# Weight sums moved into the attention on GpSimd, and the up projection's products tied in their emitted order

## The chip, the cores and the metric

The kernel runs on one core of a Trainium2 chip. The metric is the device time of one execution in microseconds (us), the median of several runs. An engine is named as in the profile: PE is TensorE, DVE is VectorE, ACT is ScalarE, POOL is GpSimd, SP issues the transfers. A name such as L191 is a line of the kernel before; the rows of the changed kernel's order carry that kernel's own lines, and the text says which line of before they answer to.

## The reference

One layer of a decoder trunk over 1040 tokens (16 learned ones and 1024 given ones) of 1024 features:

```python
h = layer_norm(concat([meta, x]))
proj = h @ w_in
q_lat, kv_lat, k_pe, z, xbc, dt_raw, g_attn, g_ssd = split(proj)
y_attn = mla_branch(q_lat, kv_lat, k_pe, ...)     # 8 heads, softmax(q k) v, then @ w_o
y_ssd  = ssd_branch(z, xbc, dt_raw, ...)          # chunked state-space scan, then @ w_o_ssd
mixed  = sigmoid(g_attn) * y_attn + sigmoid(g_ssd) * y_ssd
h = layer_norm(ALPHA * h + mixed @ w_out)
u = causal_dwconv(h @ w_up)                        # D_FF = 2816: 22 gate and 22 value tiles of 128
gate, val = split(u)
h = layer_norm(ALPHA * h + (silu(gate) * val) @ w_down)
return h[:, 16:]
```

All inputs are float32. Every large product is made of three products of rounded parts (a high and a low part of each operand: high by high, low by high, high by low).

## The kernel before, in words

The kernel runs through stages one after the other: embedding norm and latents (0 to 155 us of the span), the attention (to 541), the gate stage (to 752), the state-space stage (to 1420), its output products and the merged output product (to 1751), the up projection (to 2232) and the down projection. Activations lie with features on the 128 partitions and tokens along the free axis. Instructions are written per stage in Python; a scheduler then sets each engine's order from their emitted order, their priorities and the tiles that are free. An engine runs its own list strictly in that order, and SP issues nearly all transfers in one list.

**Attention.** Eight heads (`hd`), three column chunks of 348 tokens (`c`). For each of these 24 units `scores` makes the score tiles in PSUM, the maximum (L571), the exponential on ACT, and scales the tile `p` on DVE (L589); the last block of a tile is filled with zeros on GpSimd (L593, a memset). `weighted` of the unit before transposes the `p` tiles on PE (L611) and multiplies them with the values (L617). The head's weights are loaded (`wraw<-wk`, `wraw<-wqb`) and split by ACT and DVE.

**Gate stage.** For each of eight blocks `m`: `o_proj` and `gate` (L698 on DVE) with their products on PE; after block 2 `dt_chain`, which for three chunks runs a chain of some 16 small DVE instructions on a 64-partition tile `q` (L719 to L733, one buffer), and ends in three transposes of `q` on PE (L736); `h_centered`, a column sum of eight tiles on DVE (L760) with one product on PE (L762); and `down_sums`, called two at a time. `down_sums(j)` (L738 to L749), for 11 values of `j`, loads two 512 KB blocks of the down projection's weights (tiles `tw1`, `tw2`, one buffer each), makes four differences of 128x512 on DVE and stores both blocks again (`t13_d[j]`, `t42_d[j]`). Only the down projection reads them.

**Up projection.** It is a blocked product with seven products (q = 1 to 7) of half size in place of eight. `prod(ps, q, w)` is one of them: 24 matmuls of 128x258 or 128x256 (L191) into a PSUM pair `d`. The right operands are forms of the normalized activations, four tiles each: `T1`, `T2`, `T3`, `T4`, `B2` for q = 5, 6, 7, 4, 3; each form is a cast on ACT (L199) and a difference on DVE (L200). The left operands are made per tile pair `f` (22 of them) by `wrest(f)`: two weight loads of 512 KB, four sums `s1` to `s4` of 128x512 on GpSimd (L1108 to L1111), and splits by ACT and DVE. `first(f)` calls `wrest` and issues product 6 of the first four `f` (products 1 and 2 of these stand earlier, beside the norm), with `u2 = p1 + d` on DVE (L1148); the loop over `f` then emits products 7, 5, 3, 4. In between stand the convolution steps on DVE and ACT (`conv_up`, L1131 and L1133).

**The norm before it.** `rs` is a list of eight tiles of the residual (`r` in the rows). The lines from L1191 on make `T2` (with the temporary tile `t2`), then `rs[j] = rs[j+4] - rs[j]` (L1196) and the forms `T3`, `T1`, `B2`; then four blocks `b21` are loaded back from DRAM (`b<-h_d`), reduced by `t2` on GpSimd (L1205), and formed into `T4`. Then `first(0)` and the loop.

## Time and profile before

| | |
|---|---|
| time, median of 3 runs | 2474.98 us (2471.23 to 2476.71) |
| the profiled execution's own time | 2476.96 us |
| its span, first to last instruction | 2474.9 us |
| mean granted TensorE clock | 0.986 of full speed |
| PE busy | 2379.6 us (96%), 16319 matmuls |
| DVE busy | 1746.3 us (71%), 3945 instructions |
| ACT busy | 1137.5 us (46%) |
| POOL busy | 202.2 us (8%), 190 instructions |
| chain that ended last | PE 80%, DVE 8%, DMA 6%, issue 2%, ACT 2%, POOL 1% |

The span is 2.06 us shorter than the execution's time; that rest lies before the first and after the last instruction. Shares are means over the whole span, so they say little of one stage. A PE window of 62 us in the up projection that holds no idle time has 516 matmuls.

### The profile page before, as it was taken

How to read it: one execution, taken by the hardware profiler on the slowest of the kernel's cores; microseconds unless marked ns; L12 is line 12 of the kernel's file. 1: busy time of each engine (PE TensorE's matmuls, PEld its weight loads, DVE VectorE, ACT ScalarE, POOL GpSimd, SP SyncE). 2: the span in 40 equal slices, each digit the busy share in tenths (PEclk: the TensorE clock that was granted, in tenths of full speed). 3: DMA queues.
4: the chain of work that ended last, by engine and by line, in shares of the span. 5: the costliest groups of instructions: out<-in, count | busy, mean ns of one | idle time of the engine just before them, and what ended most of it. 6: DMA issues, size and time to landing. Idle time of an engine off the chain costs nothing.

```text
span 2474.9 us, 42581 instructions
## 1 busy us (share of the span) xinstructions
PE 2379.6 (96%) x16319; PEld 2252.3 (91%) x16319; DVE 1746.3 (71%) x3945; ACT 1137.5 (46%) x2481; POOL 202.2 (8%) x190
## 2 busy tenths in 40 slices
PE   6999999999999999999999999999789999999996
PEld 5998988989999999999999999999789999998885
DVE  6467667676767678776877744855778777766858
ACT  5335545562226555445554432432544444445443
POOL 0000000000000000000000000202332222210004
PEclk9999999999999999999999999999899999999998
DMA  6120110147792312222212254644322222229332
GB/s 205 47 66 29 42 38 26 46 137 254 246 308 85 101 64 87 82 79 89 84 64 82 66 176 139 212 154 148 116 86 81 83 83 81 78 85 304 123 111 98
DMA packets 124620, 277.29 MB, mean 112 GB/s; under 512 B 14720, under 2 KB 49792, under 8 KB 122368
## 3 DMA queue, kind: packets, MB, share of 16 engines
q1 hardware_dynamic: 124416, 274.57, 33.8%
q8 instruction: 128, 2.10, 0.3%
q14 instruction: 76, 0.62, 0.1%
HBM read 209.62 MB, written 62.80 MB: 110 GB/s over the span
## 4 chain that ended last, share of the span: by engine, by line
PE 80%; DVE 8%; DMA 6%; issue 2%; ACT 2%; POOL 1%; SPq 0%; DVEq 0%; ACTq 0%; POOLq 0%
PE d L191 25%; PE g L171 11%; PE g L173 11%; PE g L172 11%; PE g L1339 5%; PE c L617 3%; PE c L1339 2%; PE c L908 2%; PE c L611 1%; PE c L932 1%; PE c L912 1%; DMA yl<-y_d 1%; DMA tw<-wdl 1%; DMA wraw<-wup 1%; DVE wl L161 1%
## 5 line engine op out<-in xcount | busy, mean ns | idle before, releaser
L191 PE MATMUL d<-f,wh 128*128 128x258 f32 (+1 forms) x4000 | 655.5, 286 | 28.2 <-DVE u L1148 15.7
L191 PEld LDWEIGHTS d<-f,wh 128*128 128x128 f32 x4000 | 558.7, 192 | 31.0 <-ACT wh L199 20.0
L171 PE MATMUL g<-h,wh 128*128 128x348 f32 (+3 forms) x1560 | 508.0, 326 | 4.7 <-ACT lat L399 4.7
L172 PE MATMUL g<-h,wl 128*128 128x348 f32 (+3 forms) x1560 | 507.4, 325 | 0.0
L173 PE MATMUL g<-h,wh 128*128 128x348 f32 (+3 forms) x1560 | 507.0, 325 | 0.0
L191 PE MATMUL d<-f,wl 128*128 128x258 f32 (+1 forms) x2000 | 407.6, 285 | 6.1 <-DVE wl L200 4.3
L191 PEld LDWEIGHTS d<-f,wl 128*128 128x128 f32 x2000 | 314.4, 192 | 7.9 <-DVE wl L200 5.5
L171 PEld LDWEIGHTS g<-h,wh 128*128 128x128 f32 x1560 | 295.4, 189 | 7.4 <-ACT lat L399 5.0
L172 PEld LDWEIGHTS g<-h,wl 128*128 128x128 f32 x1560 | 295.8, 190 | 2.7 <-issue 2.7
L173 PEld LDWEIGHTS g<-h,wh 128*128 128x128 f32 x1560 | 295.1, 189 | 2.7 <-issue 2.7
L161 DVE TENSOR_TENSOR wl<-wraw,wh 128x512 fp32r<-128x512 f32 (+2 forms) x278 | 193.6, 698 | 142.1 <-ACT wh L160 138.9
L160 ACT CAST wh<-wraw 128x512 fp32r<-128x512 f32 (+2 forms) x278 | 167.1, 604 | 254.8 <-PE d L191 122.6
L171 PE MATMUL g<-a,wh 128*128 128x348 f32 (+2 forms) x456 | 149.2, 328 | 1.9 <-DVE kn L200 1.1
L172 PE MATMUL g<-a,wl 128*128 128x348 f32 (+2 forms) x456 | 148.1, 325 | 0.0
L173 PE MATMUL g<-a,wh 128*128 128x348 f32 (+2 forms) x456 | 147.8, 324 | 0.0
L200 DVE TENSOR_TENSOR wl<-wraw,wh 128x512 fp32r<-128x512 f32 x136 | 99.6, 741 | 60.3 <-ACT wh L199 60.2
L199 ACT CAST wh<-wraw 128x512 fp32r<-128x512 f32 x136 | 82.7, 617 | 106.5 <-DMA wraw<-wup 48.9
L813 DVE SCALAR_TENSOR_TENSOR xc<-g,V,xc 128x347 f32<-128x347 f32 (+2 forms) x180 | 103.5, 576 | 33.0 <-ACT xc L809 30.2
L898 ACT ACTIVATE G<-ac,tok 116x116 f32<-116x116 f32 x288 | 91.6, 379 | 42.5 <-PE c L908 42.5
L1339 PE MATMUL g<-wh,dh 128*128 128x512 f32 x352 | 110.7, 396 | 0.0
L1133 DVE SCALAR_TENSOR_TENSOR va<-u,V,va 128x512 f32<-128x512 f32 x88 | 94.8, 1077 | 20.4 <-ACT va L1131 19.1
L199 ACT CAST wh<-s 128x512 fp32r<-128x512 f32 x88 | 53.9, 617 | 88.2 <-PE d L191 45.6
(306 smaller groups left out, 4216.0 us busy)
## 6 DMA issues: line engine op xcount, KB each, us to landing
wraw<-win SPq DMA_DIRECT2D x65, 512.0 KB, 3.4
wraw<-wup SPq DMA_DIRECT2D x48, 512.0 KB, 3.4
ac<-cs_d SPq DMA_DIRECT2D x16, 1044.0 KB, 5.7
wraw<-wos SPq DMA_DIRECT2D x32, 512.0 KB, 3.9
tw<-wdl SPq DMA_DIRECT2D x22, 512.0 KB, 4.6
t_d<-tw SPq DMA_DIRECT2D x22, 512.0 KB, 3.1
gv<-gv_d SPq DMA_DIRECT2D x44, 256.0 KB, 5.9
wraw<-t_d SPq DMA_DIRECT2D x44, 256.0 KB, 3.4
```

The source lines that it names most:

```text
L160: nc.scalar.copy(h[:, :n * ncol], r)
L161: nc.vector.tensor_sub(l[:, :n * ncol], r, f32(h[:, :n * ncol]))
L171: nc.tensor.matmul(ps, ah, bh, start=(k == 0), stop=False)
L172: nc.tensor.matmul(ps, al, bh, start=False, stop=False)
L173: nc.tensor.matmul(ps, ah, bl, start=False, stop=(k == n - 1))
L191: ins = nc.tensor.matmul(ps[:, PO + c0:PO + c1], a, b[:, c0:c1], start=(start and k == 0 and i == 0), stop=(k == n - 1 and i == 2), skip_g ...
L199: nc.scalar.copy(H, src)
L200: nc.vector.tensor_sub(L, src, f32(H))
L813: nc.vector.scalar_tensor_tensor(t[:, l:n], ps[:, hal + l - s:hal + n - s], vec("cw", (3 - s) * 24 + ct), t[:, l:n], ALU.mult, ALU.add)
L898: nc.scalar.activation(G_[:, k * S:(k + 1) * S], ac[:S, hh, C0[b] + k * S:C0[b] + (k + 1) * S], AF.Relu, bias=tok[:, 3 * b + k, 32 + hd:33 ...
L1133: nc.vector.scalar_tensor_tensor(t, src[:, 2 - k:HN - k], vec("fw", (2 - k) * 44 + ti), t, ALU.mult, ALU.add)
L1339: nc.tensor.matmul(pss[t], a[:, o], b, start=(first and j == 0 and i == 0), stop=(j == KH - 1 and i == 2), skip_group_check=not first)
```

## The change

It has three parts.

First, `down_sums` leaves the gate stage and is called in the attention, in each second unit, on GpSimd in place of DVE, with a pool of its own of two buffers per tile. Loads, stores, sums and their number (11 times two loads, four differences, two stores) are the same.

Second, `prod` ties each product behind the one emitted before it (`issue_after`), so that the scheduler can't mix or exchange products; in the loop `first` of a later `f` is emitted just ahead of product 3. The split weights of q = 4 change pool with those of q = 3, and `u2`, `u4` lie in another pool than the rest.

Third, the forms of the second norm are made in their order of use: `T3`, then the loads of `b21` into tiles that the residual leaves free, `T1` with the `b21` differences on DVE in place of GpSimd, then `first(0)`, and only then `B2` and `T4`.

```diff
@@ -642,6 +642,21 @@
                 split(H[:, :n], L[:, :n], of[:, :n])
                 oh[k][c] = (H[:, :n], L[:, :n])
+    pds = eB.enter_context(pool("DS", 2))
+
+    def down_sums(j):
+
+        x, y = (pds.tile([P, D], F32, name=k, tag=k) for k in ("tw1", "tw2"))
+        nc.sync.dma_start(x, wdl[j])
+        nc.sync.dma_start(y, wdl[j + KH])
+        (b11, b12), (b21, b22) = ((t[:, :512], t[:, 512:]) for t in (x, y))
+        nc.gpsimd.tensor_sub(b11, b12, b11)
+        nc.gpsimd.tensor_sub(b12, b22, b12)
+        nc.gpsimd.tensor_sub(b22, b22, b11)
+        nc.gpsimd.tensor_sub(b21, b21, b22)
+        nc.sync.dma_start(t13_d[j], x)
+        nc.sync.dma_start(t42_d[j], y)
+
     last = None
     for hd in range(HEADS):
@@ -657,6 +672,9 @@
                     others()
             if c == 0 and hd % 2 == 0:
                 vt = values(hd // 2)
+            unit = 3 * hd + c
+            if unit % 2 == 0 and unit // 2 < KH:
+                down_sums(unit // 2)
             last = (hd, c, Pt, vt)
     weighted(*last)
@@ -735,19 +753,6 @@
                 for k in range(3):
                     nc.tensor.transpose(tp[:S, k * 64:(k + 1) * 64], q[:, k * S:(k + 1) * S], ident[:64, :64])
                 nc.scalar.copy(tok[:, 3 * c:3 * c + 3, :], tp[:S, :192].rearrange("p (a b) -> p a b", b=64))
-        def down_sums(j):
-
-            x, y = (p3.tile([P, D], F32, name=k, tag=k) for k in ("tw1", "tw2"))
-            nc.sync.dma_start(x, wdl[j])
-            nc.sync.dma_start(y, wdl[j + KH])
-            (b11, b12), (b21, b22) = ((t[:, :512], t[:, 512:]) for t in (x, y))
-            nc.vector.tensor_sub(b11, b12, b11)
-            nc.vector.tensor_sub(b12, b22, b12)
-            nc.vector.tensor_sub(b22, b22, b11)
-            nc.vector.tensor_sub(b21, b21, b22)
-            nc.sync.dma_start(t13_d[j], x)
-            nc.sync.dma_start(t42_d[j], y)
-
         def h_centered(c):
             n = C1[c] - lo(c)
@@ -779,9 +784,6 @@
             gate(B_GA, m, m1_d, yat)
             if m == 2:
                 dt_chain()
-            for j in range(2 * m - 2, 2 * m):
-                if 0 <= j < KH:
-                    down_sums(j)
             if m > 2 and m - 3 < 3:
                 h_centered(m - 3)
             if m + 3 < KT:
@@ -975,7 +977,9 @@
     eF = ctx.enter_context(ExitStack())
     pf1 = eF.enter_context(pool("F1", 16))
     eD = ctx.enter_context(ExitStack())
-    p = eD.enter_context(pool("Dr", 1, "right"))
+    prr = eD.enter_context(pool("Dr", 8, "right"))
+    eT = ctx.enter_context(ExitStack())
+    p = eT.enter_context(pool("Dt", 1, "right"))
     eM = ctx.enter_context(ExitStack())
     pyh = eM.enter_context(pool("Dy", 33, "right"))
     pm = eM.enter_context(pool("Dm", 17, "right"))
@@ -1013,7 +1017,7 @@
     wm = p.tile([P, KT, 1], F32, name="wm", bufs=1)
     for k in range(KT):
         for q in range(2):
-            raw = dtmp("wr", "r", 8)
+            raw = ftile(prr, F32)
             nc.sync.dma_start(raw[:, :512], wor[k][:, 512 * q:512 * q + 512])
             nc.vector.reduce_sum(wm2[:, k, q:q + 1], raw[:, :512], axis=AX.X)
     nc.vector.tensor_add(wm, wm2[:, :, 0:1], wm2[:, :, 1:2])
@@ -1059,7 +1063,7 @@
             W = load_w(wout[m], KT, center=wm)
             ps = dpair()
             mm3h(ps, W, mix)
-            r, hr = dtmp("r", "r", 8), dtmp("hr", "ml", 3)
+            r, hr = ftile(prr, F32), dtmp("hr", "ml", 3)
             nc.sync.dma_start(hr, hc_d[m][:, cols(hi)])
             nc.vector.scalar_tensor_tensor(r, hr, ALPHA, half(ps), ALU.mult, ALU.add)
             if m == 0:
@@ -1072,7 +1076,7 @@
     eM.close()
     pf2 = eF.enter_context(pool("F2", 40))
     p0 = eF.enter_context(pool("E0", 1))
-    pz = eD.enter_context(pool("Dz", hB, "right"))
+    pz = eT.enter_context(pool("Dz", hB, "right"))
@@ -1113,17 +1117,24 @@
             if w is None:
                 r.update({1: wsplit(wp, a11, 4), 2: wsplit(wp, a12, 4)})
             for q, a in ((4, a22), (7, s3), (6, s2), (5, s1), (3, s4)):
-                r[q] = wsplit(p0, a, 4) if q in (7, 6, 3) else wsplit(pe[0], a, 3)
+                r[q] = wsplit(p0, a, 4) if q in (4, 7, 6) else wsplit(pe[0], a, 3)
             return r
+    order = []
+
     def prod(ps, q, w, start=True):
-        return mm3h(ps, w[q], rhs[q], start)
+
+        with tc.issue_after(order[0]) if order else ExitStack():
+            ins = mm3h(ps, w[q], rhs[q], start)
+        order[:] = [ins.ins]
+        return ins
     pe = []
     def etile(name, bufs):
-        return (p0 if name in ("p1", "c11") else pe[0]).tile([P, HN], F32, name=name, tag=name, bufs=bufs)
+        pl = p0 if name in ("p1", "c11") else pe[0] if name in ("u2", "u4") else pe[1]
+        return pl.tile([P, HN], F32, name=name, tag=name, bufs=bufs)
     def conv_up(src, ti, tag, bufs):
@@ -1195,26 +1206,28 @@
     for j in range(hB):
         nc.vector.tensor_sub(rs[j], rs[j + hB], rs[j])
         T3[j] = form(pf2, rs[j])
+    b21 = []
+    for j in range(hB):
+        b21.append(ftile(prr, F32))
+        nc.sync.dma_start(b21[j], h1_d[j + hB][:, cols(0)])
     for j in range(hB):
         T1[j] = form(pf2, b11[j])
     for j in range(hB):
+        nc.vector.tensor_sub(b21[j], b21[j], t2[j])
+    rhs.update({5: T1, 6: T2, 7: T3})
+    eT.close()
+    pe.append(eF.enter_context(pool("E1", 1)))
+    first(0)
+    for j in range(hB):
         B2[j] = form(pf2, rs[j + hB])
     for j in range(hB):
-        b21 = dtmp("b21", "r", 8)
-        nc.sync.dma_start(b21, h1_d[j + hB][:, cols(0)])
-        nc.gpsimd.tensor_sub(b21, b21, t2[j])
-        T4[j] = form(pf2, b21)
-    rhs.update({3: B2, 4: T4, 5: T1, 6: T2, 7: T3})
-
+        T4[j] = form(pf2, b21[j])
+    rhs.update({3: B2, 4: T4})
     eD.close()
-    pe.append(eF.enter_context(pool("E1", 1)))
-    first(0)
+    pe.append(eF.enter_context(pool("E2", 1)))
     begun = 1
     for f in range(NFF):
         q = st[f]
-        while begun < min(NHEAD, f + 2):
-            first(begun)
-            begun += 1
         w, x0, p1 = q["w"], q["x0"], q["p1"]
         x2 = dpair()
         prod(x2, 7, w)
@@ -1237,7 +1250,7 @@
             nc.scalar.copy(u4, half(x0))
         nc.vector.tensor_add(u4, u4, half(x2))
         vb = conv_up(u4, f + NFF, "va", 2)
-        while begun < min(NFF, f + (3 if f + 1 < NHEAD else 2)):
+        if begun < NFF:
             first(begun)
             begun += 1
         prod(x0, 3, w, False)
```

How the orders move, in the attention, the gate stage and the up projection. In these rows the names carry buffer numbers, which differ between the two kernels.

**GpSimd in the attention.** Before, its list holds only the memsets of the `p` tiles:

```order
L593 MEMSET p_2011 111x107
L593 MEMSET p_2030 111x112
L593 MEMSET p_2300 115x1
L593 MEMSET p_2346 115x2
L593 MEMSET p_2584 111x107
L593 MEMSET p_2603 111x112
```

In the changed kernel the differences of `down_sums` (L653 to L656, L744 to L747 of before) stand between them:

```order
L653 TENSOR_TENSOR tw1_2839<-tw1_2839 128x512
L654 TENSOR_TENSOR tw1_2839<-tw2_2840,tw1_2839 128x512
L593 MEMSET p_2313 115x1
L653 TENSOR_TENSOR tw1_3475<-tw1_3475 128x512
L593 MEMSET p_2359 115x2
L654 TENSOR_TENSOR tw1_3475<-tw2_3476,tw1_3475 128x512
L655 TENSOR_TENSOR tw2_3476<-tw2_3476,tw1_3475 128x512
L656 TENSOR_TENSOR tw2_3476<-tw2_3476 128x512
L653 TENSOR_TENSOR tw1_3791<-tw1_3791 128x512
L654 TENSOR_TENSOR tw1_3791<-tw2_3792,tw1_3791 128x512
L593 MEMSET p_2607 111x107
L655 TENSOR_TENSOR tw2_3792<-tw2_3792,tw1_3791 128x512
```

The memset that was the fourth of the list (`p_2346`, now `p_2359`) has 13 differences ahead of it, and all 44 stand ahead of the list's 10th memset (each head has four).

**SP in the attention**, the changed kernel, from the first stores of `down_sums` (L657, L658) on:

```order
L657 DMA t13_d0_122<-tw1_2143 128x1024
L658 DMA t42_d0_133<-tw2_2144 128x1024
L147 DMA wraw_2469<-wk 128x256
L147 DMA wraw_2508<-wqb 128x768
L651 DMA tw2_2460<-wdl 128x1024
L650 DMA tw1_2839<-wdl 128x1024
L651 DMA tw2_2840<-wdl 128x1024
L657 DMA t13_d1_123<-tw1_2459 128x1024
L658 DMA t42_d1_134<-tw2_2460 128x1024
L657 DMA t13_d2_124<-tw1_2839 128x1024
L658 DMA t42_d2_135<-tw2_2840 128x1024
L147 DMA wraw_3029<-wqb 128x768
```

The weights of the next heads (`wraw<-wk`, `wraw<-wqb`, L147) stand behind these stores, which wait for GpSimd. Before, nothing but loads and the stores of head results stood there.

**DVE in the gate stage**, at `dt_chain`'s second chunk (`q` is its tile; `tw1`, `tw2` are those of `down_sums`), before:

```order
L745 TENSOR_TENSOR tw1_8342<-tw2_8343,tw1_8342 128x512
L161 TENSOR_TENSOR wl_8242<-wraw_8235,wh_8241 128x512
L698 SCALAR_TENSOR_TENSOR ga_8011<-ga_8011,ya_7520 128x344
L719 TENSOR_SCALAR q_8057<-w_8056 64x348
L746 TENSOR_TENSOR tw2_8343<-tw2_8343,tw1_8342 128x512
L721 SCALAR_TENSOR_TENSOR q_8057<-q_8057,w_8056 64x348
L747 TENSOR_TENSOR tw2_8343<-tw2_8343 128x512
L721 SCALAR_TENSOR_TENSOR q_8057<-q_8057,w_8056 64x348 x6
L722 SCALAR_TENSOR_TENSOR q_8057<-q_8057,u_8055 64x348
```

and in the changed kernel (L737 to L739 answer to L719 to L721, L716 to L698):

```order
L716 SCALAR_TENSOR_TENSOR ga_8047<-ga_8047,ya_7580 128x334
L716 SCALAR_TENSOR_TENSOR ga_8076<-ga_8076,ya_7607 128x348
L161 TENSOR_TENSOR wl_8312<-wraw_8309,wh_8311 128x512
L737 TENSOR_SCALAR q_8151<-w_8150 64x348
L739 SCALAR_TENSOR_TENSOR q_8151<-q_8151,w_8150 64x348
L161 TENSOR_TENSOR wl_8316<-wraw_8309,wh_8315 128x512
L716 SCALAR_TENSOR_TENSOR ga_8105<-ga_8105,ya_7634 128x344
L739 SCALAR_TENSOR_TENSOR q_8151<-q_8151,w_8150 64x348 x6
L740 SCALAR_TENSOR_TENSOR q_8151<-q_8151,u_8149 64x348
```

The chain no longer has differences with loads ahead of it or in it; on PE its transposes now stand 11 matmuls earlier than before.

**DVE at the start of the up projection**, before, from the last `T1` forms on (then `B2` and `T4`):

```order
L200 TENSOR_TENSOR f_20951<-f_20866,f_20950 128x514
L200 TENSOR_TENSOR f_20955<-f_20868,f_20954 128x514
L200 TENSOR_TENSOR f_20959<-r_20364,f_20958 128x514
L200 TENSOR_TENSOR f_20963<-r_20431,f_20962 128x514
L200 TENSOR_TENSOR f_20967<-r_20498,f_20966 128x514
L200 TENSOR_TENSOR f_20971<-r_20565,f_20970 128x514
L200 TENSOR_TENSOR f_20978<-b21_20974,f_20977 128x514
L200 TENSOR_TENSOR f_20985<-b21_20981,f_20984 128x514
L200 TENSOR_TENSOR f_20992<-b21_20988,f_20991 128x514
L200 TENSOR_TENSOR f_20999<-b21_20995,f_20998 128x514
L1148 TENSOR_TENSOR u2_21064<-p1_20618,d_21039 128x514
L200 TENSOR_TENSOR wl_21020<-wraw_21009,wh_21019 128x512
```

and in the changed kernel (L1216 is the `b21` difference, L1159 answers to L1148):

```order
L200 TENSOR_TENSOR f_20946<-f_20304,f_20945 128x514
L1216 TENSOR_TENSOR f_20949<-f_20949,t2_20884 128x514
L200 TENSOR_TENSOR f_20958<-f_20869,f_20957 128x514
L1216 TENSOR_TENSOR f_20951<-f_20951,t2_20897 128x514
L200 TENSOR_TENSOR f_20962<-f_20871,f_20961 128x514
L1216 TENSOR_TENSOR f_20953<-f_20953,t2_20910 128x514
L200 TENSOR_TENSOR f_20966<-f_20873,f_20965 128x514
L1216 TENSOR_TENSOR f_20955<-f_20955,t2_20923 128x514
L200 TENSOR_TENSOR f_20970<-f_20875,f_20969 128x514
L200 TENSOR_TENSOR f_21042<-f_20371,f_21041 128x514
L1159 TENSOR_TENSOR u2_21039<-p1_20625,d_21014 128x514
L200 TENSOR_TENSOR wl_21007<-s1_20986,wh_21006 128x512
L200 TENSOR_TENSOR wl_21011<-s4_20989,wh_21010 128x512
```

`u2` now stands ahead of the last three `B2` forms and of the `T4` forms. On PE, before, product 6 of f = 0 (into `d_21039`) is followed by its products 5 and 3, and 7 (`d_21125`) comes after these:

```order
L191 MATMUL d_21039<-f_20919,wh_21027 128x258
L191 MATMUL d_21039<-f_20919,wh_21027 128x256
L191 MATMUL d_21039<-f_20942,wh_21031 128x258
...
L191 MATMUL d_21039<-f_20955,wh_21031 128x258
L191 MATMUL d_21039<-f_20955,wh_21031 128x256
L191 MATMUL d_21039<-f_20958,wh_21035 128x258
L191 MATMUL d_21039<-f_20958,wh_21035 128x256
...
L191 MATMUL d_21125<-f_20923,wh_21023 128x258
L191 MATMUL d_21125<-f_20923,wh_21023 128x256
```

In the changed kernel product 6 (`d_21014`) is followed by 7 (`d_21077`), then 5, then product 6 of f = 1 (`d_21170`):

```order
L191 MATMUL d_21014<-f_20926,wh_21002 128x258
L191 MATMUL d_21014<-f_20926,wh_21002 128x256
L191 MATMUL d_21077<-f_20930,wh_20998 128x258
...
L191 MATMUL d_21077<-f_20946,wh_20998 128x258
L191 MATMUL d_21077<-f_20946,wh_20998 128x256
L191 MATMUL d_21014<-f_20957,wh_21006 128x258
L191 MATMUL d_21014<-f_20957,wh_21006 128x256
...
L191 MATMUL d_21170<-f_20886,wh_21158 128x258
L191 MATMUL d_21170<-f_20886,wh_21158 128x256
```

Products 3 and 4 of f = 0 follow behind that.

## Rows read from the trace of the kernel before

**Rows 1.** Windows of 62 us, core 0, from the output product to the up projection.

```profile
core 0: us, PE busy (x) PEld busy (x) DVE busy (x) ACT busy (x) POOL busy (x), PEclk, DMA share, GB/s
1736.00:1798.00 62.00, 45.25 (x355) 44.16 (x354) 48.96 (x77) 34.39 (x58) 16.69 (x8) 0.85 0.33 111
1798.00:1860.00 62.00, 53.03 (x415) 51.18 (x414) 47.50 (x62) 24.88 (x40) 23.49 (x16) 0.99 0.23 77
1860.00:1922.00 62.00, 59.78 (x481) 59.44 (x480) 50.34 (x66) 29.06 (x47) 18.29 (x13) 0.97 0.28 94
1922.00:1984.00 62.00, 62.00 (x516) 62.00 (x515) 48.01 (x63) 29.88 (x49) 16.65 (x12) 1.00 0.25 77
```

**Rows 2.** TensorE's waits by line waited for, whole span: total, times, longest.

```profile
PE d L191 <- DVE u L1148: 15.7, 1, 15.7
...
PE c L736 <- DVE q L733: 3.6, 2, 3.4
...
PE c L762 <- DVE hs L760: 2.1, 1, 2.1
```

**Rows 3.** Windows of 10 us in the gate stage, columns as in Rows 1.

```profile
630.00:640.00 10.00, 6.64 (x35) 6.23 (x34) 8.86 (x21) 2.27 (x5) 0.00 (x0) 0.79 0.74 247
640.00:650.00 10.00, 10.00 (x58) 10.00 (x57) 7.65 (x13) 1.88 (x4) 0.00 (x0) 0.87 0.60 227
660.00:670.00 10.00, 10.00 (x66) 10.00 (x65) 4.44 (x11) 2.48 (x5) 0.00 (x0) 1.00 0.96 309
700.00:710.00 10.00, 7.94 (x42) 7.22 (x41) 5.71 (x12) 1.88 (x4) 0.00 (x0) 0.88 0.85 275
```

**Rows 4.** Timeline of the gate stage, VectorE: start, length, idle before and releaser.

```profile
624.10 0.69 DVE L744 TENSOR_TENSOR tw<-tw 128x512 f32<-128x512 f32 x1 [3.37 <-DMA tw<-wdl]
...
628.70 0.33 DVE L719 TENSOR_SCALAR q<-w 64x348 f32<-64x348 f32 x1
...
706.32 0.69 DVE L744 TENSOR_TENSOR tw<-tw 128x512 f32<-128x512 f32 x1 [2.20 <-DMA tw<-wdl]
```

**Rows 5.** Timeline of TensorE there.

```profile
636.92 0.57 PE L736 MATMUL c<-K,q 64*116 64x64 f32 x3 [3.36 <-DVE q L733]
```

**Rows 6.** Timeline of TensorE at the start of the up projection.

```profile
1793.97 0.77 PE L191 MATMUL d<-f,wh 128*128 128x258 f32 x2 [15.73 <-DVE u L1148]
```

**Rows 7.** Timeline of VectorE there.

```profile
1781.22 2.50 DVE L200 TENSOR_TENSOR f<-f 128x514 fp32r<-128x514 f32 x4
...
1787.95 5.28 DVE L200 TENSOR_TENSOR f<-b,f 128x514 fp32r<-128x514 f32 x4 [1.81 <-ACT f L199]
```

**Rows 8.** Timeline of GpSimd there.

```profile
1781.67 10.18 POOL L1205 TENSOR_TENSOR b<-b,t 128x514 f32<-128x514 f32 x4 [7.81 <-DMA b<-h_d]
1798.03 1.28 POOL L1108 TENSOR_TENSOR s<-wraw 128x512 f32<-128x512 f32 x1 [6.19 <-DMA wraw<-wup]
```

**Rows 9.** DMA issues, 1760 to 1800: KB each, median us to landing.

```profile
b<-h_d SPq DMA_DIRECT2D x4, 257.0 KB, 3.1
```

**Rows 10.** GpSimd's instructions by line and shape, whole span: mean ns of one.

```profile
L1111 POOL TENSOR_TENSOR s<-wraw,s 128x512 f32<-128x512 f32 x22 | 35.7, 1621 | 1.7
...
L1108 POOL TENSOR_TENSOR s<-wraw 128x512 f32<-128x512 f32 x22 | 29.4, 1337 | 95.6 <-DVE wl L200 51.4 <-DMA wraw<-wup 44.2
```

**Rows 11.** Windows in the attention, columns as in Rows 1.

```profile
153.00:255.00 102.00, 100.83 (x647) 93.39 (x647) 83.16 (x296) 51.74 (x155) 1.15 (x7) 1.00 0.19 54
...
190.00:200.00 10.00, 10.00 (x65) 8.89 (x64) 9.64 (x42) 7.23 (x25) 0.32 (x2) 1.00 0.05 19
200.00:210.00 10.00, 10.00 (x64) 9.53 (x63) 4.97 (x14) 3.02 (x7) 0.00 (x0) 1.00 0.20 57
```

**Rows 12.** Timeline of VectorE and TensorE in the attention, one softmax factor.

```profile
189.96 0.71 DVE L589 TENSOR_SCALAR p<-p,ri 116x348 f32<-116x348 f32 x2
...
195.73 0.46 PE L611 MATMUL c<-K,p 116*116 116x116 f32 x3
```

**Rows 13.** Timeline of GpSimd in the attention.

```profile
187.91 0.21 POOL L593 MEMSET p<- 115x2 f32 x1 [51.41 <-PE c L611]
```

## The prediction, as it was put on record

> **What bounds the kernel now.** I read the page's shares first: TensorE is busy 96% of the span and stands for 80% of the chain that ended last, so only a stretch in which TensorE has gaps, or in which the change makes some, can move the time. Next come the windows of the up projection. A window without gaps holds 516 matmuls, so one product of 24 takes 24 × 62/516 = 2.88 us; the three windows before it hold 355, 415 and 481 [rows 1]. The last two lack 101 + 35 = 136 matmuls, or 136 × 0.120 = 16.3 us, all in the first 125 us of this stage. The list of TensorE's waits names what the change touches: one wait of 15.7 us for `u2`, and 3.6 and 2.1 us in the gate stage [rows 2]. The windows of that stage show what such a wait costs altogether: 35, 58 and 42 matmuls in windows that could hold 66 [rows 3], with the granted clock at 0.79 and 0.87 behind the wait, so more is lost than the idle time itself. Last, the timelines of the engines that TensorE waits for. Everywhere else TensorE is full, and the attention belongs there: 100.83 of 102 us busy [rows 11]. A gain there is impossible; a loss is not.
>
> **Gate stage: the sums leave.** Forty-four VectorE differences of 0.69 us go, and more important, two places where VectorE stood in line behind their loads: 3.37 us at 624.10 and 2.20 us at 706.32 [rows 4]. At the first, `dt_chain`'s second chunk begins only at 628.70, and TensorE gets `q` 3.36 us late at 636.92 [rows 4, 5]. From L719 to the transposes that is 8.2 us, two differences (some 1.2 us) among them, so the chain itself takes about 7. In the changed order it can start at about 624.7, as soon as the transposes of the first chunk have released `q` (VectorE stands idle until 624.10 for a load that is gone then), carries a split and a gate step (1.1 us), and ends near 633. TensorE reaches the transposes 11 matmuls (11 × 0.15 = 1.7 us) earlier than it would have, at 633.56 - 1.7 = 631.9. So a wait of about 1.3 us remains of 3.36. The windows 630 to 650 lack 132 - 93 = 39 matmuls, 5.9 us; 700 to 710 lacks 24, 3.6 us. Together 9.5 us. I leave 1.3 us for the rest of the first wait and 0.7 us for `h_centered`, whose product also moves some 32 matmuls (5 us) earlier and may find its own loads late: **gain 7.5 us**, between 4 (the second place gives nothing and the first keeps its clock loss) and 9.5.
>
> **Start of the up projection.** TensorE is idle from 1778.2 to 1793.97 [rows 6]. Nothing is wrong with product 5's own operand: `u2` stands on VectorE behind all forms, the last four of which wait for GpSimd's four `b21` differences, 10.18 us from 1781.67 on, themselves behind the reload of `b21` [rows 7, 8]. In the changed order `T3` is formed first, at 1778 to 1786, and product 7 runs beside it with gaps. The last `b21` block is loaded into the tile that the last `T3` form releases, so at about 1786; it lands 3.1 us later [rows 9]; then a difference, a `T1` form, a `B2` form and `u2` at about 0.62 us each [rows 7], which gives 1791.7 for the start of product 5. That is 2.3 us earlier than now with one product (2.88 us) more behind it: 5.2 us.
>
> Behind it lie the 16.3 us of the windows up to 1922. Now the sums of the next weights start only at 1798.03 since their loads came late [rows 8]; in the changed order the weights of f = 1 are there, and products come in an order that gives each evacuation a product of time. How much of the 16.3 us this gives back I bound by VectorE's own work: 47.50 us per 415 matmuls [rows 1] is 2.75 us a product, 13.7 us for the five products of one of the first four `f`, against TensorE's 14.4. Seven forms (4.3 us) now fall into this stretch too. Over four `f` that is 59 against 57.6 us before any slowing by GpSimd: VectorE almost binds, and part of the loss stays. I take a third, 5.3 us. At one end nothing comes back, at the other all but a clock tail and a few waits of 5 us together, 11. **Gain 10.5 us**, between 5 and 16. The tie of the products costs nothing in the later `f`: a window of the steady part is already full, and its order hardly changes.
>
> **Attention: the sums arrive.** A GpSimd difference of 128x512 takes 1.34 to 1.62 us [rows 10]; 44 of them some 62 us, and GpSimd has nothing else to do there but memsets. TensorE doesn't use them before the down projection. They cost through three things. First, VectorE: four forms took 5.28 us while GpSimd ran, 1.32 each, and four like them 2.50 us, 0.62 each, while it didn't [rows 7]; so an instruction of VectorE with two inputs in SBUF that meets GpSimd takes 0.70 us longer. GpSimd's four took 2.5 us each against 1.3 [rows 8, 10]. No row shows the softmax's instructions beside GpSimd; about half of VectorE's work there reads PSUM or one SBUF tile. The ends for one sum are therefore 0 and 0.70 us, and I take half, 0.35, as nearest to that mixture: 44 × 0.35 = 15 us, at most 31, where VectorE has 102 - 83.16 = 18.8 us of idle time in all, but not evenly: 9.64 of 10 us are busy at 190 to 200, and 4.97 at 200 to 210 [rows 11]. Some 25 sums fall before 200, 8.8 us of delay, at most 17.5, where VectorE, at the 0.36 us in ten of that last row, has some 1.5 us in forty free, and the `p` tile scaled at 189.96 to 190.67 is read by TensorE at 195.73 [rows 12], 5.1 us of slack. Excess: 2 to 11 us. Second, the memsets: the one at 187.91 [rows 13] has 13 sums ahead of it, 13 × 1.4 = 18 us of them, and their loads, which the new list of SP puts at about 160; I estimate it at 198; the VectorE step that needs it stands at 195 to 199, so a few us. Third, SP's list: the weights of the next head stand behind stores that wait for GpSimd, with some 10 us in hand. I take **7 us of loss** for the three, between 0 and 20.
>
> At this place a rule speaks against the change. The Trainium skill, "SBUF — State Buffer", section "Who interferes with whom", says that a VectorE instruction with two SBUF inputs and a GpSimd instruction that reads SBUF exclude each other for a whole instruction, and that the loser blocks fully; one with a single SBUF input outside its two-port modes is not touched. The trace agrees in kind: 1.32 us in place of 0.62 [rows 7]. By the rule at its hardest every sum would hold VectorE for its 1.34 us or more, 59 us in all, in place of my 15.
>
> **Sum.** 2476.96 us for the profiled execution (2.0 above the median of 2474.98) minus 7.5 minus 10.5 plus 7 is 2466; seen from the median 2464. **Forecast 2465 us**. 0.2% of this kernel is 5 us, about what a measurement can tell from no change: faster is below 2470, slower above 2480.
>
> **Rivals.**
> *VectorE is blocked in the attention, and the kernel gets slower.* Mechanism: the sums meet two-input instructions nearly every time, 0.70 us and more each. Price: 17.5 us before 200 less 6.5 us free or slack is 11, and the remaining 19 sums add 13 us where about 10 are free, while late memsets hold VectorE's list at the next heads for some 10 us more: 23 to 28 us lost against 18 gained, about 2483. It decides from an attention loss of 23 us on. For it: 9.64 of 10 us busy [rows 11], and the row of 1.32 us. Against: the half of the work that doesn't take two SBUF tiles, and the light window at 200.
> *The start of the up projection gives nothing back after 1800, for VectorE binds there.* For it: 59 against 57.6 us. Then the gain is 5 + 7.5 against a loss of 7 to 8, about 2471: within 0.2%. The same comes out if `u2` still waits for its reload as long as now, that is, if this part of the change doesn't do what it says.
> *The attention hides the sums entirely.* For it: TensorE has 5 us of slack at the tightest row, and VectorE 18.8 us free. Loss 0 to 2, about 2458.
>
> **How the numbers follow.** The forecast's own case, a net gain of 6 to 16 us, 0.46; hidden sums 0.14; the second rival 0.24; the first 0.16. The likeliest case alone spans 2459 to 2470. The range has to reach into the second and the first rival and into the bounds of the gains (9.5 and 16 with little loss would give 2452): 2452 to 2480. Faster 0.59, same 0.25, slower 0.16.
>
> **What would show it.** In the changed profile the wait for `q` at L736's place falls to 1 or 2 us and the windows at 630 to 650 and 700 to 710 of this stage, shifted, hold 60 matmuls or more. The wait for `u2` falls to about 5 us and stands ahead of a product 5 that follows product 7; the next 124 us lack fewer than 100 matmuls, and what TensorE waits for there are VectorE's splits. In the attention, the stretch that now ends at 255 ends some 7 us later, GpSimd is busy 60 to 70 us more, and VectorE's two-input rows there have longer means than now. I am wrong if the attention grows by over 15 us, or if TensorE still stands 10 us or more ahead of product 5.

## The result, and the profile after

The changed kernel is slower: 2490.45 us (median) against 2475.85 us, ratio 1.0064, 95% interval 1.0035 to 1.0093. These are its five undisturbed runs, 2485.58 to 2501.79 us; a sixth, of 3839.04 us at a mean granted clock of 0.557, is left out. The range of the five is wider than that of before (2471.23 to 2481.05 us). The profiled execution is the fastest of them, 2485.58 us with a span of 2483.7 us, so its stages account for 8.8 us of the difference and not for all 16 (0.64%).

The ends of the stages on TensorE, each the last start of the named product in the trace (us of the span; what the stage takes longer than before in brackets):

| | before | changed |
|---|---|---|
| attention, last product with the values | 541.2 | 571.6 (+30.4) |
| gate and state-space stages, last product of its norm | 1418.3 | 1436.7 (-12.0) |
| output products, last product of the second norm's root | 1756.3 | 1770.8 (-3.9) |
| up projection, last product | 2233.6 | 2241.9 (-6.2) |
| end | 2474.9 | 2483.7 (+0.5) |

So the attention lost 30.4 us where 7 were forecast, and the three other places gained 22. The windows of the attention in the changed kernel, which answer to [rows 11]:

```profile
core 0: us, PE busy (x) PEld busy (x) DVE busy (x) ACT busy (x) POOL busy (x), PEclk, DMA share, GB/s
153.00:255.00 102.00, 86.17 (x498) 77.52 (x497) 81.13 (x227) 39.73 (x120) 46.90 (x42) 0.92 0.59 208
...
200.00:210.00 10.00, 8.66 (x56) 7.58 (x55) 9.50 (x36) 6.44 (x22) 4.77 (x5) 1.00 0.74 275
210.00:220.00 10.00, 7.45 (x25) 6.17 (x25) 7.74 (x15) 1.84 (x5) 5.63 (x6) 0.67 0.57 202
...
260.00:270.00 10.00, 6.50 (x25) 3.80 (x23) 10.00 (x19) 2.75 (x10) 8.68 (x9) 0.73 0.45 169
```

TensorE is busy 86.17 us of 102 in place of 100.83, and in two of the windows where it has gaps the granted clock is 0.67 and 0.73 of full speed. The list of TensorE's waits (total, times, longest), cut to lines of the attention, of the root of the latents' norm ahead of it (L227) and of the two other places, answers to [rows 2]:

```profile
PE c L227 <- DVE ir L240: 6.1, 6, 3.6
PE d L191 <- DVE u L1248: 5.6, 3, 2.4
PE d L191 <- DVE u L1159: 5.2, 1, 5.2
PE c L617 <- ACT ptt L616: 4.9, 4, 1.8
...
PE c L617 <- DVE ptt L614: 4.3, 3, 2.6
...
PE c L617 <- DVE ri L583: 3.5, 2, 2.7
...
PE c L754 <- DVE q L751: 0.4, 1, 0.4
```

The wait for `u2` (L1159) fell from 15.7 to 5.2 us and that for `q` from 3.6 to 0.4, as forecast. Those of L617 for what VectorE and ScalarE make of the scores are new but for 0.5 us; that of the norm's root grew from 2.5 to 6.1 us and that for `u4` (L1248) from 3.0 to 5.6. What VectorE does in the attention beside GpSimd is seen in two timelines. VectorE:

```profile
203.20 0.97 DVE L582 TENSOR_TENSOR rs<-rs,al 115x3 f32<-115x3 f32 x1
...
205.70 0.89 DVE L589 TENSOR_SCALAR p<-p,ri 115x348 f32<-115x348 f32 x3
206.51 1.24 DVE L582 TENSOR_TENSOR rs<-rs,al 115x3 f32<-115x3 f32 x1
...
208.03 0.52 DVE L571 TENSOR_REDUCE mx<-c 114x1 f32<-114x344 f32 x1
...
209.57 3.78 DVE L589 TENSOR_SCALAR p<-p,ri 115x348 f32<-115x348 f32 x3
```

and GpSimd over the same time:

```profile
202.85 1.30 POOL L653 TENSOR_TENSOR tw<-tw 128x512 f32<-128x512 f32 x1 [7.09 <-DMA tw<-wdl]
...
206.41 1.32 POOL L654 TENSOR_TENSOR tw<-tw,tw 128x512 f32<-128x512 f32 x1 [2.22 <-DMA tw<-wdl]
207.81 1.27 POOL L655 TENSOR_TENSOR tw<-tw,tw 128x512 f32<-128x512 f32 x1
209.16 1.28 POOL L656 TENSOR_TENSOR tw<-tw 128x512 f32<-128x512 f32 x1
210.39 1.37 POOL L653 TENSOR_TENSOR tw<-tw 128x512 f32<-128x512 f32 x1
211.84 1.26 POOL L654 TENSOR_TENSOR tw<-tw,tw 128x512 f32<-128x512 f32 x1
```

Three softmax factors (`x3`) take 0.89 us at 205.70, while GpSimd waits for its load; three like them at 209.57 take 3.78 us, 1.26 each, about one GpSimd difference. A product of 115 by 3 numbers (L582) takes 1.24 us at 206.51 and 0.97 at 203.20. The maximum of 344 columns out of PSUM (L571, 208.03) takes its 0.52 us as ever, right in the middle of a difference. VectorE's groups over the whole attention, count, busy time and mean, before:

```profile
L571 DVE TENSOR_REDUCE mx<-c 115x1 f32<-115x348 f32 (+5 forms) x144 | 65.4, 456 | 10.8 <-PE c L568 8.7
L589 DVE TENSOR_SCALAR p<-p,ri 115x348 f32<-115x348 f32 (+4 forms) x144 | 46.5, 366 | 1.4
...
L572 DVE TENSOR_SCALAR nm<-mx 116x1 f32<-116x1 f32 (+3 forms) x144 | 19.3, 148 | 0.8
...
L585 DVE TENSOR_SCALAR ri<-al,ri 116x2 f32<-116x2 f32 (+2 forms) x48 | 10.8, 225 | 0.5
...
L582 DVE TENSOR_TENSOR rs<-rs,al 116x2 f32<-116x2 f32 (+2 forms) x48 | 7.5, 156 | 0.4
...
L580 DVE TENSOR_REDUCE nm<-nm 116x1 f32<-116x2 f32 (+2 forms) x48 | 7.0, 146 | 0.0
```

and changed:

```profile
L571 DVE TENSOR_REDUCE mx<-c 115x1 f32<-115x348 f32 (+5 forms) x144 | 65.1, 455 | 10.5 <-PE c L568 8.9
L589 DVE TENSOR_SCALAR p<-p,ri 115x348 f32<-115x348 f32 (+4 forms) x144 | 60.5, 463 | 1.4
...
L572 DVE TENSOR_SCALAR nm<-mx 116x1 f32<-116x1 f32 (+3 forms) x144 | 19.1, 147 | 0.8
...
L585 DVE TENSOR_SCALAR ri<-al,ri 116x2 f32<-116x2 f32 (+2 forms) x48 | 13.3, 276 | 0.5
...
L582 DVE TENSOR_TENSOR rs<-rs,al 116x2 f32<-116x2 f32 (+2 forms) x48 | 11.4, 237 | 0.3
...
L580 DVE TENSOR_REDUCE nm<-nm 116x1 f32<-116x2 f32 (+2 forms) x48 | 7.0, 146 | 0.0
```

L589 costs 14.0 us more, L582 3.9, L585 2.5; L571, L572 and L580 nothing. The trace tells which instructions GpSimd holds up. All 13 factors (L589) that start more than 0.1 us before the end of a running difference take 0.99 to 1.48 us, against 0.39 in the median of the others. Beside them, all 12 such scalings of a single column (L572), 6 reductions of two or three columns (L580) and 10 additions with one input in PSUM (L570) keep their length (at most 0.15, 0.15 and 0.29 us).

### The profile page after: what moved, and what is told of

It reads as the page before. It is cut to its first block, busy times and chain, and to the rows that moved or that the text cites. A ratio compares the mean times of both kernels' runs of the same rounds, so it can differ in the third digit from the quotient of the medians.

```text
span 2483.7 us, 42662 instructions
## 1 busy us (share of the span) xinstructions
PE 2389.0 (96%) x16319; PEld 2258.5 (91%) x16319; DVE 1737.4 (70%) x3905; ACT 1138.4 (46%) x2481; POOL 255.9 (10%) x230
## 4 chain that ended last, share of the span: by engine, by line
PE 82%; DVE 9%; DMA 3%; issue 2%; ACT 1%; POOL 1%; SPq 0%; DVEq 0%; ACTq 0%; POOLq 0%
PE d L191 24%; PE g L173 12%; PE g L171 12%; PE g L172 12%; PE g L1352 4%; PE c L617 3%; PE c L1352 2%; PE c L910 2%; PE c L934 1%; DMA yl<-y_d 1%; PE c L914 1%; PE c L611 1%; DVE f L200 1%; DVE p L589 1%; DVE wl L200 1%
## 5 line engine op out<-in xcount | busy, mean ns | idle before, releaser
L191 PE MATMUL d<-f,wl 128*128 128x258 f32 x2000 | 407.2, 285 | 4.8 <-DVE wl L200 4.4
L617 PE MATMUL c<-ptt,v 116*128 116x344 f32 (+7 forms) x288 | 96.9, 457 | 13.3 <-ACT ptt L616 4.9
L574 ACT ACTIVATE p<-c,nm 115x348 f32<-115x348 f32 (+4 forms) x144 | 72.1, 502 | 51.1 <-DVE nm L572 40.1
```

The costliest lines, as they stand in the source:

```text
L191: ins = nc.tensor.matmul(ps[:, PO + c0:PO + c1], a, b[:, c0:c1], start=(start and k == 0 and i == 0), stop=(k == n - 1 and i == 2), skip_g ...
L617: nc.tensor.matmul(ops[:, o0:n], vt[j][:w, hh * P:(hh + 1) * P], ptt[:w, o0:n], start=(j == 0), stop=(j == nbmax - 1))
```

## The experiments

All runs were timed beside the kernel before. Each has 16319 matmuls; "lag" is how much later than in the kernel before TensorE starts the matmul of the same number, taken at the last one that the kernel before has started at 180, 250 and 540 us.

| run | ratio (95%) | attention ends | up projection takes, us | lag at 180 / 250 / 540 |
|---|---|---|---|---|
| before | 1 | 541.2 | 477.3 | 0 |
| changed | 1.0064 (1.0035 to 1.0093) | 571.6 | 471.1 | 7 / 31 / 30 |
| sums_back | 0.9969 (0.9954 to 0.9985) | 540.9 | 471.3 | 0 / 0 / 0 |
| sums_only | 1.0079 (1.0064 to 1.0095) | 571.4 | 480.0 | 8 / 31 / 30 |
| no_differences | 0.9934 (0.9916 to 0.9952) | 545.5 | 472.9 | 4 / 4 / 4 |
| differences_on_dve | 0.9943 (0.9926 to 0.9961) | 544.6 | 472.3 | 2 / 3 / 3 |
| bare_spread | 1.0150 (1.0123 to 1.0176) | 586.7 | 471.3 | 8 / 19 / 45 |
| spread | 1.0019 (1.0005 to 1.0033) | 565.7 | 471.6 | 4 / 8 / 25 |
| factor_on_act | 1.0024 (1.0013 to 1.0034) | 568.7 | 472.2 | 10 / 23 / 28 |
| factor_on_act_dve | 0.9945 (0.9929 to 0.9961) | 547.7 | 473.2 | 1 / 2 / 7 |
| spread_on_dve | 0.9959 (0.9946 to 0.9971) | 551.0 | 471.6 | 1 / 3 / 10 |
| short_differences | 1.0062 (1.0044 to 1.0080) | 574.7 | 471.6 | 10 / 31 / 34 |
| gate_on_gpsimd | 1.0053 (1.0033 to 1.0073) | 539.1 | 471.4 | -2 / -2 / -2 |
| no_ties | 0.9944 (0.9928 to 0.9959) | 546.6 | 474.6 | 3 / 5 / 5 |
| stores_on_gpsimd | 1.0061 (1.0046 to 1.0076) | 574.8 | 473.6 | 9 / 34 / 34 |
| light_head | 0.9889 (0.9872 to 0.9905) | 545.6 | 461.0 | 1 / 4 / 4 |

Two theories stood against each other for the attention. A: a GpSimd difference holds up VectorE's instructions. B: SP's list makes the next head's weights late, for stores in it wait for GpSimd. Two of the kernels below, `no_differences` and `light_head`, leave out work and so return other values; they are read for their times alone.

**The parts apart.** `sums_back` takes the first part back:

```diff
+            for j in range(2 * m - 2, 2 * m):
+                if 0 <= j < KH:
+                    down_sums(j)          # in the gate stage, on nc.vector, as before
-            if unit % 2 == 0 and unit // 2 < KH:
-                down_sums(unit // 2)      # in the attention, on nc.gpsimd
```

> The changed kernel with its first part undone: the sums of the down projection's weights again in the gate stage on VectorE, the product order and the norm's forms as changed. My theory (the attention alone loses, some 30 us; the up projection gains 6 to 10): attention ends at 541 us of the span as before, up projection ends 6 to 10 us earlier than before, total about 2468. Rival (product order and forms give nothing, or lose): 2474 or more.

`sums_only` is the kernel before with that part alone.

> The kernel before with the first part alone: sums in the attention on GpSimd, the rest untouched. My theory: attention 25 to 32 us longer, gate stage 8 to 11 us shorter, total 2491 to 2498, slower than the whole change by what the up projection gained (6 to 10 us). Rival (the three parts hinder each other through the scheduler): the attention loses clearly less here than the 30 us of the changed kernel, total below 2486.

Both came as the first theory of each said: the attention ends at 540.9 without the sums and at 571.4 with nothing but the sums. The parts roughly add up, 1.0079 and 0.9969 against 1.0064 for the whole; forms and order alone make the kernel faster.

**Which piece of the first part.** `no_differences` drops the four lines `nc.gpsimd.tensor_sub`, `differences_on_dve` turns them:

```diff
-        nc.gpsimd.tensor_sub(b11, b12, b11)
+        nc.vector.tensor_sub(b11, b12, b11)
...
```

> The changed kernel without the 44 differences (left out; loads and stores of the same blocks stay in the attention, so the down projection multiplies other weights). Theory A (GpSimd holds VectorE up instruction by instruction): attention back to within 4 us of its 541 us end, total about 2460. Theory B (SP's list and the 23 MB of transfers make the next head's weights late): attention still ends 15 us or more later than before, total 2475 or more. In between: both share.

> The changed kernel with the 44 differences of the attention on VectorE, same place, same transfers. Theory A (a VectorE instruction that meets a GpSimd difference waits out most of it, some 28 us in all): 44 x 0.69 = 30 us of VectorE time in place of it, so no better, attention end between 555 and 572, total 2478 to 2495, but the softmax factor's rows (L589) back at 0.39 us. Theory B (late weights behind stores that wait for GpSimd): stores wait less, attention ends below 553, total below 2472.

Without the differences the attention ends at 545.5, so loads and stores cost 4 of the 30 us, all of them before 180; the 26 that are left are what VectorE's rows grew by. With the differences on VectorE it ends at 544.6. I had expected no improvement from that, since 44 x 0.69 = 30 us of VectorE work come in place of some 25 us of delay. That was wrong by 10 to 27 us: work of VectorE's own in the scheduler's order costs TensorE nothing here (544.6 against 545.5 without it), while the same length of delay, put on whatever stands in line, costs all of it. By its end this run falls into B's range (below 553), and neither run tells A from B, since in both no store waits for GpSimd; the next one does. L589 is back at its mean:

```profile
L571 DVE TENSOR_REDUCE mx<-c 115x1 f32<-115x348 f32 (+6 forms) x144 | 64.6, 454 | 8.1 <-PE c L568 6.7
L589 DVE TENSOR_SCALAR p<-p,ri 115x348 f32<-115x348 f32 (+4 forms) x144 | 46.4, 365 | 1.0
```

**GpSimd by itself.** `bare_spread` leaves the real sums on VectorE in the gate stage and puts 44 GpSimd differences without loads or stores into the attention, four behind a memset:

```diff
+    for t in alone:
+        nc.gpsimd.memset(t, 1.0)
...
+            if unit % 2 == 0 and unit // 2 < KH:
+                with after_last(zeroed), after_last(stored):   # behind the last memset of a p tile; stored stays empty
+                    sums_alone()                  # four nc.gpsimd.tensor_sub on tiles of their own
```

> The kernel of the run sums_back (sums in the gate stage on VectorE) with 44 further differences of 128x512 on GpSimd in the attention, on tiles of their own that nobody reads, without any load or store, four behind a memset of every second unit, so spread over the eight heads. It tells GpSimd's instructions apart from the stores and loads in SP's list. Theory A (each difference holds VectorE up by 0.6 us): some 25 us more VectorE time over 385 us, where it has some 90 us free; TensorE loses 5 to 15 us of it; total 2474 to 2486, and rows of L589 over 1 us beside GpSimd. Theory B (SP's list, late weights): nothing lost, 2468 to 2473.

The attention ends at 586.7, 45 us late, three times the most that I expected and far above 2486 in the total (2514.81), with nothing in SP's list: A is shown by itself. The first group of four differences (1.3 us each) stands beside the root of the latents' norm and costs 8 us; each of the other ten costs 2 to 5. Right behind a memset VectorE has just come to the factors, and 33 of them run beside a difference (count, busy time and mean up to 560 us; L594 is the factor here, L576 the maximum):

```profile
L594 DVE TENSOR_SCALAR p<-p,ri 115x348 f32<-115x348 f32 (+4 forms) x133 | 74.6, 603 | 1.4
L576 DVE TENSOR_REDUCE mx<-c 115x1 f32<-115x348 f32 (+4 forms) x136 | 61.4, 453 | 9.8 <-PE c L573 8.9
```

`spread` puts the real sums there, loads behind the stores of head results.

> The changed kernel with the sums on GpSimd spread: four behind a memset of every second unit, loads behind a store of a head's result, so over all eight heads in place of the first three. Theory A: the same 25 to 28 us of VectorE time, but where it has more free time: attention ends at 550 to 560, total 2468 to 2480. If the loss per difference is what counts, not the density: attention ends at 565 or later, total as changed.

It ends at 565.7 and keeps some 25 of the 30 us: the density matters little, my 550 to 560 was too hopeful. `spread_on_dve` has the same places on VectorE.

> As the run spread, with the differences on VectorE (loads behind the stores of head results). It would be the best if the 3.4 us that the attention still loses in differences_on_dve come from the density of transfers and differences at its start: attention ends at 541 to 544, total 2459 to 2463. If not: as differences_on_dve, 2463 to 2466.

551.0 is later than the 544.6 of the sums placed freely, not earlier: the scheduler's own places were better than those that I tied.

**The instruction that grew most.** `factor_on_act` moves L589 to ScalarE, and `factor_on_act_dve` is its control:

```diff
-                nc.vector.tensor_scalar(pts[z][:m, :kc], pts[z][:m, :kc], ri[:m, z:z + 1], None, ALU.mult)
+                nc.scalar.activation(pts[z][:m, :kc], pts[z][:m, :kc], AF.Identity, scale=ri[:m, z:z + 1])
```

> The changed kernel with the softmax factor (L589, 144 instructions with one input in SBUF, which beside GpSimd grew most, by 14 us in sum) on ScalarE, all else as changed. Theory A: about half of the loss goes with it: attention ends at 553 to 562, total 2475 to 2486; ScalarE's rows of it stay near one duration beside GpSimd. Theory B: the end stays at 568 or later.

> Control for factor_on_act: differences on VectorE as in differences_on_dve, and the softmax factor on ScalarE. What it loses against differences_on_dve (attention end 544.6 us) is the price of the move to ScalarE by itself. If that is 10 us or more (end 555 or later), factor_on_act did take away half of GpSimd's harm and paid it back on ScalarE; if the end is below 550, the harm moved to VectorE's other instructions.

568.7 is not what A let me expect (553 to 562) and lies in B's range by its end. But the move alone costs 3.1 us (547.7 against 544.6), and with GpSimd's sums the end comes 2.9 us earlier, so taking away the group with half of the delay gave 6 us of 30. Part of the rest went on to the next VectorE instructions in line, L585 and L582, which grew further, from 13.3 and 11.4 us in the changed kernel:

```profile
L585 DVE TENSOR_SCALAR ri<-al,ri 116x2 f32<-116x2 f32 (+2 forms) x48 | 14.9, 310 | 0.8
L582 DVE TENSOR_TENSOR rs<-rs,al 116x2 f32<-116x2 f32 (+2 forms) x48 | 14.1, 295 | 11.5 <-ACT al L581 9.7 <-ACT p L574 1.5
```

**Shorter differences.** `short_differences` cuts each into four of 128x128:

```diff
-        nc.gpsimd.tensor_sub(b11, b12, b11)
...
+        for a, b, o in ((b12, b11, b11), (b22, b12, b12), (b22, b11, b22), (b21, b22, b21)):
+            for s in range(0, 512, P):
+                nc.gpsimd.tensor_sub(o[:, s:s + P], a[:, s:s + P], b[:, s:s + P])
```

> The changed kernel with each of the 44 GpSimd differences of 128x512 cut into four of 128x128, same elements, same place. If a VectorE instruction waits until the GpSimd instruction that is running has ended (Theory A in its narrow form), the wait per meeting falls to about a third: rows of L589 with at most 0.8 us in place of 1.5, attention end at 548 to 560, total 2465 to 2478. If GpSimd's total time next to VectorE is what counts, nothing is won: attention end 568 or later, total 2488 or more.

The rows follow the narrow form of A, the time doesn't: the attention ends at 574.7, where 548 to 560 was expected. Three factors that meet short differences take 1.36 us, 0.45 each, and the longest of all 144 takes 0.67 us against 1.55 in the changed kernel. But one split waited through a run of short differences, 2.87 us (VectorE, then GpSimd):

```profile
209.64 1.36 DVE L589 TENSOR_SCALAR p<-p,ri 115x348 f32<-115x348 f32 x3
...
220.27 2.87 DVE L200 TENSOR_TENSOR qn<-rt,qn 128x348 fp32r<-128x348 f32 x1 [0.55 <-ACT qn L199]
```

```profile
209.86 3.61 POOL L655 TENSOR_TENSOR tw<-tw,tw 128x128 f32<-128x128 f32 x8 [3.67 <-DMA tw<-wdl]
...
218.53 2.56 POOL L655 TENSOR_TENSOR tw<-tw,tw 128x128 f32<-128x128 f32 x6
221.06 1.28 POOL L655 TENSOR_TENSOR tw<-tw 128x128 f32<-128x128 f32 x3
```

and GpSimd is busy longer in all (81 us with 176 pieces in place of 58), so stores are later and the next head's weights with them. SP's list, then TensorE:

```profile
222.79 0.32 SPq L657 DMA_DIRECT2D t_d<-tw  x1
...
224.46 0.48 SPq L147 DMA_DIRECT2D wraw<-wqb  x1
```

```profile
233.17 1.51 PE L617 MATMUL c<-ptt,v 116*128 116x344 f32 x2 [7.97 <-ACT ptt L616]
```

These 8 us are theory B's wait: ScalarE, which makes `ptt`, waits 9.04 us for those weights before it. In the changed kernel's attention the only wait for a head's weights is one of 0.84 us on ScalarE at 200.56.

**B tried directly.** `stores_on_gpsimd` changes `nc.sync.dma_start` to `nc.gpsimd.dma_start` in the two stores.

> The changed kernel with the 22 stores of the sums issued by GpSimd's own queue, so that SP's list no longer waits for GpSimd; the differences stay on GpSimd in the attention. If VectorE's meetings with GpSimd make the loss: attention ends at 566 to 576 as in the changed kernel (571.6). If SP's list has a share: it ends 5 us or more earlier.

574.8 against 571.6: nothing won. The run is not clean, though: the stores take GpSimd some 13 us to issue, and the factors (L589) grow to 71.3 us from 60.5, so a gain from a shorter SP list could be hidden behind more of A. That B has no visible share in the changed kernel's loss rests on its trace, the one wait of 0.84 us.

**Another stage.** `gate_on_gpsimd` has the sums in the gate stage, on GpSimd.

> The sums back in the gate stage, there on GpSimd; product order and forms as changed. It tells whether GpSimd differences cost as much beside other VectorE work (splits with two SBUF inputs, the chain of dt_chain). Theory A: 44 x 0.6 us of VectorE delay here too, the chain's 348-column instructions among them, so no better than sums_back: 2470 to 2485. If the harm is special to the attention: VectorE is rid of 30 us, 2460 to 2466.

It is slower than the kernel before, 1.0053 (2489.69 us, above the 2485 that I expected at most), against 0.9969 with the same sums on VectorE. The largest single wait of that stage is for the most part not a meeting but B: `dt_chain`'s third load stands in SP's list behind a store that waits for GpSimd, and is issued at 641.53, where `sums_back` issues it at 634.44 (SP's list, then TensorE):

```profile
641.16 0.33 SPq L747 DMA_DIRECT2D t_d<-tw  x1
641.53 0.46 SPq L711 DMA_DIRECT2D xx<-dt_d  x1
```

```profile
663.74 0.57 PE L735 MATMUL c<-K,q 64*116 64x64 f32 x3 [11.47 <-DVE q L732]
```

The chain that then runs on VectorE meets differences as well; its product L716 of 64 by 344 numbers takes 1.59 us, where `sums_back` has 0.50.

**The up projection.** `no_ties` drops `issue_after` in `prod` from `differences_on_dve`; `light_head` leaves out two VectorE steps of the convolution for the first four tile pairs there:

```diff
-        for k in (1, 2):
+        for k in (1, 2) if ti % NFF >= NHEAD else ():
             nc.vector.scalar_tensor_tensor(t, src[:, 2 - k:HN - k], vec("fw", (2 - k) * 44 + ti), t, ALU.mult, ALU.add)
```

> The run differences_on_dve without the tie of the products. The scheduler's order of products is then the same up to product 5 of f = 1, and mixes some later ones. The up projection's gain of 6 us comes from the forms' order, not from the tie, and VectorE binds behind it: total within 3 us of 2464. Rival (the tie keeps TensorE from waiting later): 4 us or more slower, 2468 to 2475.

> The run differences_on_dve with the two VectorE steps of the convolution left out for the first four tile pairs (32 instructions of 0.75 us, 24 us; the convolution there keeps one tap of three). If VectorE binds at the start of the up projection: the part from the end of the second norm's root to the end of the up projection falls from 472 us to 458 to 467, total 2450 to 2459. If something else binds (loads, ScalarE, the clock): 470 or more, total 2461 or more.

Without the tie the up projection takes 474.6 us in place of 472.3 and the total is the same (0.9944 and 0.9943): the tie gives some 2 us in one trace and nothing that the totals show. With 24 us less VectorE work it takes 461.0 us, 11 less. The first windows behind the start of product 5, `differences_on_dve`:

```profile
1782.00:1844.00 62.00, 52.22 (x371) 50.76 (x372) 57.24 (x73) 28.93 (x47) 27.86 (x17) 0.89 0.27 86
1844.00:1906.00 62.00, 59.53 (x491) 59.14 (x490) 47.89 (x64) 28.39 (x46) 16.18 (x12) 1.00 0.26 86
```

and `light_head`:

```profile
1780.00:1842.00 62.00, 56.45 (x425) 55.62 (x426) 44.89 (x57) 32.38 (x52) 28.64 (x19) 0.91 0.28 94
1842.00:1904.00 62.00, 62.00 (x515) 62.00 (x515) 42.13 (x57) 29.99 (x48) 17.05 (x12) 1.00 0.26 86
```

371 matmuls become 425 and 491 become 515, with VectorE's 57.24 us down to 44.89.

## Why the prediction was wrong

*What bounds the kernel* held: only TensorE's gaps moved the time, and the attention, full before, could only lose.

*The attention, 7 us of loss with 20 as the bound* is the step that failed: it was 30.4, of which loads and stores alone cost 4 and the differences 26. The count of 44 and the length of a difference (1.33 us, as forecast) were right. Wrong was the price of one, "0 and 0.70 us, and I take half, 0.35", and the premise behind it, that VectorE's work on PSUM or on one SBUF tile is not held up. For PSUM it held. But the factor L589 has one SBUF tile, and its meetings cost 14 of the some 26 us by which VectorE's rows grew (L589 14.0, L582 3.9, L585 2.5, and splits and the norm's small steps). So 0.6 us a difference, near the upper end that I had set, and made otherwise than I had it: against the medians of before, 33 VectorE instructions are held up by more than 0.1 us, 0.8 us each in the mean, so fewer and longer than 44 times half of 0.70. The Trainium skill, "SBUF — State Buffer", section "Who interferes with whom", counts tensor_scalar among the instructions that can enter a two-port mode, where their operands allow it, and then contend, and leaves reductions out. The rows agree, though they don't show a mode: 1.26 us in place of 0.30 for L589, no change for the reductions L571 and L580. I had drawn on that section's lines on two inputs and on one input outside these modes, and had not asked which of the two L589 is. The second error is that I set the delay against VectorE's idle time. `differences_on_dve` shows that 30 us of ordinary work do fit into that idle time (544.6) and `bare_spread` that delay does not (586.7): it falls on the instructions that TensorE will want next, and behind such gaps the granted clock is lower as well, 0.67 of full speed in the window at 210. I had also not looked ahead of the first head: 9 us of the lag arise from 150 to 175, part of them in the root of the latents' norm (L227), whose steps on 128 by 3 numbers stood beside the first differences. One that took 0.17 us at 148.15 takes this at 154.07 (VectorE, then GpSimd):

```profile
154.07 1.22 DVE L236 TENSOR_SCALAR iv<-iv 128x3 f32<-128x3 f32 x1
...
153.97 1.30 POOL L654 TENSOR_TENSOR tw<-tw,tw 128x512 f32<-128x512 f32 x1
```

My second and third cause, listed as equals, show next to nothing in the changed kernel: in its attention TensorE, VectorE and ScalarE wait for no memset, and 0.84 us for a head's weights. What makes the 4 us of the loads and stores is open.

*The gate stage, 7.5 us with 9.5 as the upper end,* was right in its mechanism and at its upper end: up to the first product of the state-space stage TensorE needs 199.6 us in place of 209.0, 9.4 less, as the wait for `q` went to 0.4 us and not to 1.3, and that for `hs` is gone from the list. The other 2.6 of the 12.0 us lie in the state-space stage, which the prediction left out; at its start the wait for `ct` fell from 1.7 to 0.4 us.

*The start of the up projection, 10.5 us.* Its first term held: product 5 starts 4.0 us earlier in its stage (after 33.7 us in place of 37.7 from the root's last product) behind one product more, 6.9 us against a forecast of 5.2, and TensorE waits 5.25 us there. The second term, a third of 16.3 us, was nothing: the window behind it holds 390 matmuls in place of 516, with VectorE busy 58.87 of 62 us, and TensorE is full again from 1874 on (answering to [rows 1]). I had reckoned 59 us of VectorE's work for the 480 matmuls of four `f`, and so had it too small.

```profile
1812.00:1874.00 62.00, 51.34 (x390) 50.14 (x389) 58.87 (x74) 28.14 (x45) 25.85 (x16) 0.94 0.26 85
1874.00:1936.00 62.00, 62.00 (x515) 62.00 (x515) 46.36 (x63) 30.30 (x49) 16.79 (x12) 1.00 0.27 82
```

The rival that VectorE binds there was right, and `light_head` shows the bound. The 3.9 us of the output products are no forecast term and lie within the spread of that stage, 334 to 339 us over all runs.

*The rivals.* The first, slower through the attention, came true in its outcome, near the price that I had bounded it with (23 to 28 us against 30.4, "about 2483" against 2485.58 for the profiled run). Its mechanism was half right: the meetings are there, but over half of their cost is the factor with one SBUF tile and not two-input work, and the late memsets that it counted at 10 us are not seen. So that its number comes near is in part luck. I gave it 0.16: I preferred a middle between the ends of an unknown price where the one row at hand, 1.32 us in place of 0.62, stood at the upper end. Why the changed kernel's other runs are up to 16 us slower than the profiled one is open; no trace of them was read.

The best version here that leaves nothing out is the change with the differences on VectorE, with the tie or without: 2463.72 and 2463.67 us, 0.57% and 0.56% faster than before, where the 12 us of the gate and state-space stages and the up projection's 5 are kept and the attention gives back 3.4.

## What to carry to other kernels

Work moved to GpSimd next to a chain of short VectorE instructions wasn't free here, however idle GpSimd was. Count the VectorE instructions beside it that have two inputs in SBUF, or that scale an SBUF tile of more than one column, and price each meeting at up to a whole GpSimd instruction; those that read PSUM, and reductions, cost nothing in these traces. VectorE's idle time took up work that the scheduler placed, and not delay put on whatever was next in line, so compare with simply leaving the work on VectorE at a better place. And where a gap on TensorE goes, look at which engine is nearly full behind it: here VectorE, at 58.87 of 62 us, took back what the second term had promised.
